# Masked products, longer paces, and low parts of weights made by adding DMAs in a decoder trunk's first phase

## The chip, the cores and the metric

The kernel runs on one core of a Trainium2 chip. The metric is the device time of one execution in microseconds (us); less is better. TensorE (PE) multiplies matrices, VectorE (DVE), ScalarE (ACT) and GpSimd (POOL) work element by element, and SyncE (SP) issues most DMAs. Each engine runs its own queue in order and waits on semaphores of the others.

## The reference

One layer of a decoder on 512 tokens with 2048 features, all in float32:

```
u = rmsnorm(h, ln_mix);  z = u @ w_in
out_a = RG-LRU of z[:, :2048]          # 8 tiles of 128 channels: conv, two gates, a scan, norm
out_b = RWKV-7 of z[:, 2048:]          # 16 heads of 64, a recurrence over the tokens
h = h + concat(out_a, out_b) @ w_o
h = h + (gelu(conv(u @ w_gate)) * (u @ w_up)) @ w_down
h = h + rmsnorm(sigmoid(u @ w_ple_gate) * (p @ w_ple_proj));  result = rmsnorm(h)
```

The RWKV recurrence is done here in chunks of 64 tokens. In a chunk, the dependence of a token on the earlier ones is a triangular system, so each chunk of each head needs the inverse of a unit triangular 64x64 matrix.

## The kernel before

**Dense products.** Each float32 operand is split into a high part, rounded to the format that TensorE takes at full rate (float32r), and a low part, the rest. A product takes three matmuls: high by high, high by low, low by high (L151, L153, L155 in `dense`). Weights come in units, mostly 128x8x128: `wfill_` has SP load a unit to `wraw` (two buffers), ACT make the high part `whi` (L121) and DVE the low part `wlo` = raw - high (L122). There are three buffers for the pair, and units are prepared two ahead of their use. A unit of eight blocks feeds 24 matmuls of 512 columns.

**Phases.** Phase 1 does w_in, the LRU, the RWKV heads and most of w_o; phase 2 the rest of w_o, the feed-forward block and the embedding gate. The `NB` first output blocks of w_o take the first half of the RWKV rows already in phase 1 ("wob", after the point "out6", where head pair 6 must be done) and the second half in phase 2.

**Order on TensorE in phase 1.** It is written out by `merge`, which interleaves a stream of dense matmuls with generators for the eight head pairs: `prep` (decays, keys, in six steps), `batch` (scores and inverses), `chain` (the recurrence over eight chunks) and `norm`. `merge` keeps a clock t of its own. A dense matmul adds 216, and a step of a generator adds the `pe` that it yields; its next step is due when t has passed the `lat` that it yields. These come from the table `W`: `t0` after the start of the inverses, `tg` and `tt` between their levels, `lu` and `ls` in the chain, `dpace` and `pace` as the least distance of the steps of a duo (chain of pair j-1 beside batch of pair j; `dpace` for pairs 1 to 7), `g2` and `g3` for the norm, `late` and `ready` for the start of a duo, `dec` and `rsk` in prep. Since the order is fixed, TensorE waits where an operand is late, also if other matmuls could run.

**Order on the other engines.** A scheduler orders them by priority; `high_priority(offset=...)` moves a block ahead. `offw` is for the weights' conversions, `offs` for the heads' core, `offd` for what follows a dense product, `offl` for the LRU, `offt` for transposes by DVE within the core, `offp` for the steps of prep.

**Start of the inverses** (in `batch`, L755 to L762): from the scores MQ, four products (one for each group of 32 partitions) with the mask `lev1`, an add of the identity and a 32x32 transpose give Tt and Tm for the first level. The next step of TensorE on them is L768.

**Prep's second step** (L624 to L636): ACT squares k (L624), TensorE makes two small products, ACT takes tanh; `head_ss` (L905) then sums the squares on TensorE. `norm` has the same L905, GpSimd's power (L915), a copy on DVE (L917) and transposes on TensorE (L924).

Of the kernel before, what the change touches and what calls it, by code (L numbers as in the profile page):

```python
# [4 lines left out]
F32 = mybir.dt.float32  # L5
F32R = mybir.dt.float32r
AF = mybir.ActivationFunctionType
ALU = mybir.AluOpType
# [3 lines left out]
D = 2048  # L12
S = 512
KT = D // 128
NB = 6

W = dict(offw=10000, offp=[0, 5000, 1000, 2000, 5000, 5000, 1000], offl=10000, offt=100, pace=155, dpace=2794, late=4073, offs=17427, offd=2000, start=2297, lora=2383, dec=0, rsk=12597, ready=23343, bonus=39298, t0=4838, tg=1911, tt=1448, lx=14094, lu=1308, ls=1058, g1=8521, g2=4936, g3=6474, per=[2, 3, 2, 2, 2, 2, 3, 0])
DL = 1024
NP = 8
FF = 6144  # L20
# [16 lines left out]
for _n, _c in PCOLS:  # L37
# [2 lines left out]
PW = _o  # L40

CCOLS = [("ident", 128), ("ones1", 1), ("mask", 128)] + [("lev1", 32)] + [("lev%d" % b, 16) for b in (2, 4, 8, 16)] + \
        [("bdm", 128), ("bd2", 2), ("id32", 32)]
CKEEP = 129
COFF = {}
_o = 0
# [6 lines left out]
def shape_constants():  # L53
    c = np.zeros((128, CW), np.float32)
    p = np.arange(128)
    s = p % 64
    t = np.arange(64)
    c[:, COFF["ident"]:COFF["ident"] + 128] = np.eye(128)
    o = COFF["mask"]
    c[:, o:o + 64] = s[:, None] < t[None, :]  # L60
    c[:, o + 64:o + 128] = s[:, None] <= t[None, :]

    r = (p % 32)[:, None]
    t = np.arange(32)[None, :]
    c[:, COFF["lev1"]:COFF["lev1"] + 32] = (t // 2 == r // 2) & (t % 2 == 1) & (r % 2 == 0)

    for b in (2, 4, 8, 16):
        o = COFF["lev%d" % b]
        c[:, o:o + 16] = ((r // b) % 2 == 1) & (r // (2 * b) == t[:, :16] // b)
    o = COFF["id32"]  # L70
    c[:, o:o + 32] = r == t
    o = COFF["bdm"]
    c[:, o:o + 128] = (p[:, None] // 64 == p[None, :] // 64) / 64.0
    o = COFF["bd2"]
    c[:, o:o + 2] = p[:, None] // 64 == np.arange(2)[None, :]
    c[:, COFF["ones1"]] = 1.0
    return c


class Builder:  # L80
# [22 lines left out]
    def wfill_(self):  # L103
        nc = self.nc
        while self.wn < len(self.wq) and len(self.wt) < self.LOOK:
            src, shape, *own = self.wq[self.wn]
            self.wn += 1
            if callable(src):
                raw = src()
            elif self.wraw:  # L110
                raw = self.wraw.pop(0)
            else:
                raw = self.t(self.cp, "wraw", shape, bufs=self.RAW)
                nc.sync.dma_start(raw, src)
            if own:
                w = self.t(self.k2, own[0], (128, 2) + shape[1:], F32R, bufs=1)
                hi, lo = w[:, 0], w[:, 1]
            else:
                hi = self.t(self.wp, "whi", shape, F32R, bufs=self.HL)
                lo = self.t(self.wp, "wlo", shape, F32R, bufs=self.HL)  # L120
            nc.scalar.activation(hi, raw, AF.Copy)  # L121
            nc.vector.tensor_tensor(lo, raw, hi.bitcast(F32), ALU.subtract)  # L122
            self.wt.append((hi, lo))

    def wnext(self):
# [75 lines left out]
    def build(self):  # L201
        nc, tc, A = self.nc, self.tc, self.A
        self.RAW, self.HL, self.LOOK = 2, 3, 2
        self.PACE, self.OFFS, self.OFFD = W["pace"], W["offs"], W["offd"]
        from contextlib import ExitStack
        with ExitStack() as top:

            cp = top.enter_context(tc.tile_pool(name="cp", bufs=1, side="right"))
            self.cp = cp
            self.par = cp.tile([128, PW], F32, name="par")  # L210
            self.con = cp.tile([128, CKEEP], F32, name="con")
            self.mug1 = cp.tile([32, 1], F32, name="mug1")
            self.mhalf = cp.tile([128, 8], F32, name="mhalf")
            nc.gpsimd.memset(self.mhalf, -0.5)
            self.wp = top.enter_context(tc.tile_pool(name="wp", bufs=1))
            self.dp = top.enter_context(tc.tile_pool(name="dp", bufs=1, space=DRAM))
            self.bp = top.enter_context(tc.tile_pool(name="bp", bufs=1))
            self.oa = [self.dp.tile([128, S], F32, name="oa%d" % i) for i in range(8)]
            self.ob = [self.dp.tile([128, S], F32, name="ob%d" % i) for i in range(8)]
            self.rsa = cp.tile([128, S], F32, name="rsa")  # L220
            with ExitStack() as ph:
                self.pm = ph.enter_context(tc.tile_pool(name="pm1", bufs=1, space=PSUM))
                self.k1 = ph.enter_context(tc.tile_pool(name="k1", bufs=1))
                self.phase1()
            with ExitStack() as ph:
                self.pm = ph.enter_context(tc.tile_pool(name="pm2", bufs=1, space=PSUM))
                self.k2 = ph.enter_context(tc.tile_pool(name="k2", bufs=1))
                self.phase2()
# [372 lines left out]
    def prep(self, j):  # L601
        nc, A, k1 = self.nc, self.A, self.k1
        V, SC, G, TE = nc.vector, nc.scalar, nc.gpsimd, nc.tensor
# [7 lines left out]
        raw = T("lraw", 1, (128, 4, 128))  # L611
# [21 lines left out]
        SC.activation(th, th, AF.Tanh, scale=-E05 / 4, bias=self.cq[:, 0:1])  # L633
        ta = T("ta")
        SC.activation(ta, psa, AF.Tanh, scale=0.5, bias=self.dv("a0h", j))
        yield 860, W['dec']  # L636

        ss = self.head_ss(sq)
        V.tensor_scalar(th, th, -1.0, 1.0, ALU.mult, ALU.add)
# [12 lines left out]
        rsk = self.head_bc(mb)  # L652
# [10 lines left out]
        ready = self.now + W['ready']  # L663
# [10 lines left out]

        G.tensor_tensor(rt, rt, kt, ALU.mult)
        bdr = T("bdr", 1, (128, 128))
        V.tensor_scalar(bdr, self.K("bdm"), self.P("rk", j), 64.0, ALU.mult, ALU.mult)
        bv = T("bv", 2)
        self.prepped[j] = (AR, bt, ktl, vt, pc, bv, gt)
        self.ptime = max(ready, self.now + W['late'])  # L680
# [26 lines left out]
    def batch(self, j, q):  # L707
        nc, A, k1 = self.nc, self.A, self.k1
        V, SC, G, TE = nc.vector, nc.scalar, nc.gpsimd, nc.tensor
# [8 lines left out]
        MQ, NQ = T("MQ", 2, (128, NC, 128)), T("NQ", 2, (128, NC, 128))  # L718
# [36 lines left out]
        Q4 = [(slice(32 * g, 32 * g + 32), slice(32 * (g % 2), 32 * (g % 2) + 32)) for g in range(4)]  # L755
        Tm, Tt = T("Tm", 1, (128, 8, 32)), T("Tt", 1, (128, 8, 32))
        bc = lambda n, w: self.K(n).unsqueeze(1).broadcast_to([128, 8, w])
        for r_, c_ in Q4:
            V.tensor_tensor(Tt[r_], MQ[r_, :, c_], bc("lev1", 32)[r_], ALU.mult)
        V.tensor_tensor(Tt, Tt, bc("id32", 32), ALU.add)  # L760
        V.transpose(fl(Tm), fl(Tt))
        yield 2160, W['t0']  # L762

# [365 lines left out]
    def phase2(self):  # L1129
        nc, A, k2 = self.nc, self.A, self.k2  # L1130
        V, SC, G, TE = nc.vector, nc.scalar, nc.gpsimd, nc.tensor
        self.MM = 6
        self.auxtag = ("wk", 2)
        T = lambda tag, bufs=1, shape=(128, S), dt=F32: self.t(k2, tag, shape, dt, bufs)
        self.obs.append(self.last)
# [3 lines left out]
        for m in range(KT):  # L1139
# [3 lines left out]
            hi, lo = T("uh%d" % m, dt=F32R), T("ul%d" % m, dt=F32R)  # L1143
# [30 lines left out]
        raw = [None, None]  # L1174
# [145 lines left out]
        for k in range(2):  # L1320
            r = T("ld")
            nc.sync.dma_start(r, A["pT"][k])
            t_ = T("hw%d" % (4 + k), 1, (128, 2, 512), F32R)
# [178 lines left out]
```

## Time and profile before

| | us |
|---|---|
| median of 3 runs (lowest to highest) | 2706.22 (2706.09 to 2706.65) |
| profiled execution | 2707.82 |
| its span, first to last instruction | 2706.0 |
| TensorE busy | 2646.9 |
| VectorE busy | 1735.8 |
| ScalarE busy | 1051.0 |
| GpSimd busy | 291.1 |

The profile's mean granted TensorE clock is 0.99 of 2.4 GHz. A busy TensorE counts from an instruction's start to its modelled end, and consecutive matmuls overlap: a matmul of 512 columns is listed at some 390 to 400 ns. The idle time before an instruction is put down to the semaphore that ended it last ("<- engine, tile, line").

### The profile page before, as it was taken

The numbers are of one execution on the slowest core, as the hardware profiler recorded it, in microseconds if no ns is written. First come the engines' busy times: TensorE is split into PE (matmuls) and PEld (weight loads), VectorE is DVE, ScalarE is ACT, GpSimd is POOL, SyncE is SP. The second block draws the span as 40 slices with busy tenths as digits, with TensorE's granted clock in tenths as the row PEclk, the third lists the DMA queues.
The fourth block names the chain that finished last, engine by engine and source line by source line (L and its number), as shares of the span: only waits on it lengthen the run. The fifth ranks groups of instructions, "written<-read, shape, count | busy, mean of one in ns | idle before, by whom it ended". The sixth has DMA issues, their size and how long they took to land.

```text
span 2706.0 us, 43401 instructions
## 1 busy us (share of the span) xinstructions
PE 2646.9 (98%) x18440; PEld 2175.3 (80%) x18440; DVE 1735.8 (64%) x2321; ACT 1051.0 (39%) x1483; POOL 291.1 (11%) x217
## 2 busy tenths in 40 slices
PE   8999999999999999999999999999999999999996
PEld 7877777787787788888888888888888888888886
DVE  7774866677574634666666667667666667775235
ACT  6453454446432433333333333333333333335244
POOL 4010110101121310000000000000000000000013
PEclk9999999999999999999999999999999999999998
DMA  5221221222242422323323323232233323332322
GB/s 174 90 75 57 83 75 52 80 83 68 91 141 75 133 93 86 102 99 107 100 101 109 102 94 107 93 104 95 100 109 101 109 94 101 101 107 85 101 86 102
DMA packets 81890, 261.35 MB, mean 97 GB/s; under 512 B 9504, under 2 KB 12192, under 8 KB 81696
## 3 DMA queue, kind: packets, MB, share of 16 engines
q1 hardware_dynamic: 81696, 258.58, 28.9%
q8 instruction: 144, 2.36, 0.4%
q14 instruction: 50, 0.41, 0.0%
HBM read 250.42 MB, written 8.13 MB: 96 GB/s over the span
## 4 chain that ended last, share of the span: by engine, by line
PE 90%; DVE 5%; ACT 2%; POOL 1%; issue 1%; DMA 1%; SPq 0%; DVEq 0%; POOLq 0%
PE wk L1171 12%; PE wk L1170 12%; PE wk L1172 12%; PE mm L155 7%; PE mm L153 7%; PE mm L151 7%; PE mm L1253 6%; PE mm L1252 6%; PE mm L1254 6%; PE mm L1341 2%; PE mm L1339 2%; PE mm L1340 2%; PE wk L768 2%; PE mm L1170 1%; PE mm L1172 1%; PE mm L1171 1%
## 5 line engine op out<-in xcount | busy, mean ns | idle before, releaser
L121 ACT ACTIVATE whi<-wraw 128x1024 fp32r<-128x1024 f32 (+2 forms) x361 | 375.2, 1039 | 744.6 <-PE mm L153 195.7
L122 DVE TENSOR_TENSOR wlo<-wraw,whi 128x1024 fp32r<-128x1024 f32 (+2 forms) x361 | 444.7, 1232 | 225.9 <-ACT whi L121 220.2
L1170 PE MATMUL wk<-uh,whi 128*128 128x512 f32 x1408 | 547.8, 389 | 0.0
L1171 PE MATMUL wk<-ul,whi 128*128 128x512 f32 x1408 | 547.7, 389 | 0.0
L1172 PE MATMUL wk<-uh,wlo 128*128 128x512 f32 x1408 | 547.7, 389 | 0.0
L121 ACT ACTIVATE whi<-hw 128x1024 fp32r<-128x1024 f32 x154 | 163.3, 1061 | 464.5 <-PE wk L1171 418.5
L151 PE MATMUL mm<-xh,whi 128*128 128x512 f32 x832 | 333.7, 401 | 1.5 <-DVE y L888 0.9
L155 PE MATMUL mm<-xh,wlo 128*128 128x512 f32 x832 | 333.6, 401 | 1.5 <-DVE wlo L122 1.5
L153 PE MATMUL mm<-xl,whi 128*128 128x512 f32 x832 | 333.2, 401 | 0.0
L1172 PEld LDWEIGHTS wk<-uh,wlo 128*128 128x128 f32 x1408 | 264.3, 188 | 54.9
L1170 PEld LDWEIGHTS wk<-uh,whi 128*128 128x128 f32 x1408 | 264.3, 188 | 54.9
L1171 PEld LDWEIGHTS wk<-ul,whi 128*128 128x128 f32 x1408 | 264.3, 188 | 54.8
L122 DVE TENSOR_TENSOR wlo<-hw,whi 128x1024 fp32r<-128x1024 f32 x154 | 188.7, 1225 | 181.0 <-ACT whi L121 178.5
L1253 PE MATMUL mm<-wlo,hid 128*128 128x512 f32 x680 | 265.1, 390 | 0.0
L1254 PE MATMUL mm<-whi,hid 128*128 128x512 f32 x680 | 264.8, 389 | 0.0
L1252 PE MATMUL mm<-whi,hid 128*128 128x512 f32 x680 | 264.8, 389 | 0.0
L1198 POOL TENSOR_TENSOR tmp<-tmp,rsa 128x512 f32<-128x512 f32 x48 | 87.4, 1821 | 1361.0 <-ACT tmp L1197 1361.0
L151 PEld LDWEIGHTS mm<-xh,whi 128*128 128x128 f32 x832 | 158.5, 190 | 37.4 <-issue 3.7
L155 PEld LDWEIGHTS mm<-xh,wlo 128*128 128x128 f32 x832 | 158.0, 190 | 37.3 <-issue 2.8
L153 PEld LDWEIGHTS mm<-xl,whi 128*128 128x128 f32 x832 | 158.4, 190 | 34.2 <-issue 1.3
L1267 DVE TENSOR_TENSOR h<-h,mm 128x512 f32<-128x512 f32 x264 | 175.2, 682 | 0.6
L1252 PEld LDWEIGHTS mm<-whi,hid 128*128 128x128 f32 x680 | 127.6, 188 | 26.4
(468 smaller groups left out, 3648.3 us busy)
## 6 DMA issues: line engine op xcount, KB each, us to landing
wraw<-wgu SPq DMA_DIRECT2D x192, 512.0 KB, 3.2
hw<-wd SPq DMA_DIRECT2D x88, 512.0 KB, 3.2
wraw<-wz SPq DMA_DIRECT2D x80, 512.0 KB, 3.5
wraw<-wpg SPq DMA_DIRECT2D x31, 512.0 KB, 3.2
wraw<-wo SPq DMA_DIRECT2D x24, 512.0 KB, 3.4
wraw<-wo SPq DMA_DIRECT2D x16, 256.0 KB, 2.8
tmp<-xT SPq DMA_DIRECT2D x16, 256.0 KB, 2.8
wraw<-wd SPq DMA_DIRECT2D x8, 512.0 KB, 3.2
```

What stands on the lines that cost most here:

```text
L121: nc.scalar.activation(hi, raw, AF.Copy)
L122: nc.vector.tensor_tensor(lo, raw, hi.bitcast(F32), ALU.subtract)
L151: nc.tensor.matmul(ps, hi[:, k, :], xh, start=first and i == 0, stop=False)
L153: nc.tensor.matmul(ps, hi[:, k, :], xl, start=False, stop=False)
L155: nc.tensor.matmul(ps, lo[:, k, :], xh, start=False, stop=last and i == n - 1)
L1170: TE.matmul(ps, wh[:, k, :], xh, start=h + k == 0, stop=False)
L1171: TE.matmul(ps, wh[:, k, :], xl, start=False, stop=False)
L1172: TE.matmul(ps, wl[:, k, :], xh, start=False, stop=h == 1 and k == 7)
L1252: TE.matmul(ps, x[0][:, k, ts_], w[0][:, k, :], start=first and k == 0, stop=False)
L1253: TE.matmul(ps, x[0][:, k, ts_], w[1][:, k, :], start=False, stop=False)
L1254: TE.matmul(ps, x[1][:, k, ts_], w[0][:, k, :], start=False, stop=last and k == 1)
L1267: V.tensor_tensor(o, o, ps[tt], op)
```

## The change

Five things change.

1. The start of the inverses takes two products on all 128 partitions instead of four on 32. Each has a mask by partition (`odd`, a new constant of two columns) beside `lev1`; an add of the identity and an add of the two results follow. Also, `bdr` is made from `bd2`, and the constant `bdm` is dropped.
2. `NB` goes from 6 to 8, so two more half blocks of w_o are done in phase 1.
3. The table `W` has new values: longer `t0`, `dpace`, `ls`, `late`, `lora`, `g3`, `pace`, shorter `tg` and `start`, and other offsets for the priorities.
4. A new `dec7` is the distance between prep's second and third step for the last head pair, where `dec` is 0 for all others.
5. In phase 1 (`acc_lo`), every other unit of shape 128x8x128 gets its low part in another way: ACT writes the negated high part to `wlo`, and a DMA issued by GpSimd adds the weights from DRAM to it. DVE has no part in it. Space for GpSimd's DMA descriptors is doubled.

```
-NB = 6
-W = dict(offw=10000, offp=[0, 5000, 1000, 2000, 5000, 5000, 1000], offl=10000, offt=100, pace=155, dpace=2794, late=4073, offs=17427, offd=2000, start=2297, lora=2383, dec=0, rsk=12597, ready=23343, bonus=39298, t0=4838, tg=1911, tt=1448, lx=14094, lu=1308, ls=1058, g1=8521, g2=4936, g3=6474, per=[2, 3, 2, 2, 2, 2, 3, 0])
+NB = 8
+W = dict(offw=3000, offp=[0, 300, 0, 1000, 5000, -100, 466], offl=0, offt=0, pace=1007, dpace=3159, late=8560, offs=10000, offd=3000, start=1554, lora=5885, dec=0, rsk=12832, ready=23343, bonus=39298, t0=5900, tg=1601, tt=1464, lx=4233, lu=1319, ls=1435, g1=97321, g2=4936, g3=7972, per=[2, 3, 2, 2, 2, 2, 3, 0], dec7=6140)
...
+    c[:, COFF["odd"]:COFF["odd"] + 2] = p[:, None] // 32 % 2 == np.arange(2)[None, :]
...
             nc.scalar.activation(hi, raw, AF.Copy)
-            nc.vector.tensor_tensor(lo, raw, hi.bitcast(F32), ALU.subtract)
+            if self.acc_lo and not callable(src) and shape == (128, 8, 128) and self.wn % 2:
+                nc.scalar.activation(lo, hi.bitcast(F32), AF.Copy, scale=-1.0)
+                nc.gpsimd.dma_start(lo, src, accum_op=ALU.add)
+            else:
+                nc.vector.tensor_tensor(lo, raw, hi.bitcast(F32), ALU.subtract)
...
-        yield 860, W['dec']
+        yield 860, W['dec'] if j < NP - 1 else W['dec7']
...
-        V.tensor_scalar(bdr, self.K("bdm"), self.P("rk", j), 64.0, ALU.mult, ALU.mult)
+        V.tensor_scalar(bdr.rearrange("p (h f) -> p h f", h=2), self.K("bd2").unsqueeze(2).broadcast_to([128, 2, 64]), self.P("rk", j), None, ALU.mult)
...
-        for r_, c_ in Q4:
-            V.tensor_tensor(Tt[r_], MQ[r_, :, c_], bc("lev1", 32)[r_], ALU.mult)
-        V.tensor_tensor(Tt, Tt, bc("id32", 32), ALU.add)
+        for i, t_ in enumerate((Tm, Tt)):
+            V.scalar_tensor_tensor(t_, MQ[:, :, 32 * i:32 * i + 32], self.K("odd")[:, i:i + 1], bc("lev1", 32), ALU.mult, ALU.mult)
+        V.tensor_tensor(Tm, Tm, bc("id32", 32), ALU.add)
+        V.tensor_tensor(Tt, Tt, Tm, ALU.add)
         V.transpose(fl(Tm), fl(Tt))
...
-    nc = _bacc.Bacc("TRN2", target_bir_lowering=False, num_devices=1, dynamic_dma_scratch_size=512)
+    nc = _bacc.Bacc("TRN2", target_bir_lowering=False, num_devices=1, dynamic_dma_scratch_size=1024)
```

## Rows read from the trace of the kernel before

**Rows 1.** Stretches: start:end, length, busy of PE PEld DVE ACT POOL; clock, DMA.
```profile
36.00:890.00 854.00, 823.53 (x10094) 656.23 (x10094) 562.08 (x944) 388.84 (x639) 112.17 (x87) 0.98 0.26 81
890.00:2686.00 1796.00, 1791.83 (x8153) 1491.60 (x8151) 1131.78 (x1331) 629.88 (x783) 149.88 (x93) 1.00 0.30 101
```

**Rows 2.** Waits of PE, 44 to 890 us: total us, times, longest us.
```profile
PE wk L768 <- DVE Tm L761: 6.8, 2, 5.1
PE wk L768 <- DVE us L849: 3.3, 2, 2.1
PE wk L905 <- ACT tmp L624: 3.0, 1, 3.0
PE wk L924 <- DVE Sq L917: 2.9, 1, 2.9
PE wk L924 <- DVE MQ L728: 1.8, 2, 1.1
...
PE mm L155 <- DVE wlo L122: 1.5, 1, 1.5
...
PE wk L726 <- DVE bt L657: 0.9, 1, 0.9
```

**Rows 3.** Stretches around three of the six places of low clock.
```profile
317.00:321.50 4.50, 4.50 (x86) 3.78 (x87) 3.98 (x7) 0.09 (x1) 3.43 (x3) 0.62 0.27 81
...
733.50:741.50 8.00, 7.57 (x23) 6.37 (x24) 6.35 (x10) 1.43 (x2) 1.64 (x1) 0.57 0.20 45
...
884.00:891.00 7.00, 5.57 (x15) 4.24 (x16) 3.19 (x5) 1.44 (x2) 0.04 (x1) 0.51 0.04 16
```

**Rows 4.** PE in order of time (start us, us): dense matmuls three apart.
```profile
879.78 0.39 PE L155 MATMUL mm<-xh,wlo 128*128 128x512 f32 x1
...
880.46 0.40 PE L155 MATMUL mm<-xh,wlo 128*128 128x512 f32 x1
```

**Rows 5.** Groups of DVE by line, 36 to 890 us: count, busy us, mean ns.
```profile
L759 DVE TENSOR_TENSOR Tt<-MQ,con 32x256 f32<-32x256 f32 x32 | 13.8, 430 | 0.5
...
L760 DVE TENSOR_TENSOR Tt<-Tt,con 128x256 f32<-128x256 f32 x8 | 3.2, 406 | 0.1
```

**Rows 6.** DVE in order of time: one scalar_tensor_tensor.
```profile
494.29 0.74 DVE L442 SCALAR_TENSOR_TENSOR kt<-zs,par,tmp 128x512 f32<-128x512 f32 x1
```

**Rows 7.** PE in order of time, chunks of the last chain ahead of "out6".
```profile
853.31 0.33 PE L847 MATMUL ch<-st,MQ 64*64 64x64 f32 x4 [0.21 <-DVE st L870]
853.47 0.28 PE L853 MATMUL ch<-vk,kk 64*64 64x64 f32 x4
...
855.30 0.33 PE L847 MATMUL ch<-st,MQ 64*64 64x64 f32 x4 [0.88 <-DVE st L870]
```

**Rows 8.** Groups by line, 36 to 860 us: the conversions of weights.
```profile
L121 ACT ACTIVATE whi<-wraw 128x1024 fp32r<-128x1024 f32 x97 | 102.6, 1058 | 151.1 <-PE mm L153 143.9 <-issue 5.3 <-PE ch L862 0.8
...
L122 DVE TENSOR_TENSOR wlo<-wraw,whi 128x1024 fp32r<-128x1024 f32 x97 | 129.0, 1330 | 32.5 <-ACT whi L121 31.5 <-PE wk L193 0.5 <-PE mm L155 0.2
```

**Rows 9.** DMA issues, 50 to 860 us: count, KB each, median us to landing.
```profile
wraw<-wz SPq DMA_DIRECT2D x75, 512.0 KB, 3.5
```

**Rows 10.** Groups of POOL by line, 36 to 860 us: its longest op.
```profile
L983 POOL TENSOR_TENSOR lxl<-lxl,lrc 128x512 f32<-128x512 f32 x4 | 8.4, 2106 | 27.2 <-DVE us L849 9.2 <-ACT bk L746 6.9 <-DVE lrc L598 6.4
```

**Rows 11.** ACT and PE in order of time: two units, high part and low part's use.
```profile
30.80 1.06 ACT L121 ACTIVATE whi<-wraw 128x1024 fp32r<-128x1024 f32 x1 [1.20 <-DMA wraw<-wz]
...
36.55 0.40 PE L155 MATMUL mm<-xh,wlo 128*128 128x512 f32 x1
...
473.30 1.07 ACT L121 ACTIVATE whi<-wraw 128x1024 fp32r<-128x1024 f32 x1
...
481.72 0.39 PE L155 MATMUL mm<-xh,wlo 128*128 128x512 f32 x1
```

**Rows 12.** DVE and POOL in order of time, 481 to 484 us.
```profile
481.60 2.04 DVE L122 TENSOR_TENSOR wlo<-wraw,whi 128x1024 fp32r<-128x1024 f32 x1
...
481.27 1.29 POOL L983 TENSOR_TENSOR lt<-lt,lrc 128x512 f32<-128x512 f32 x1 [7.21 <-ACT lxl L977]
```

More of the change, by code (lines that the diff above doesn't have):

```diff
@@ L42 @@
 CCOLS = [("ident", 128), ("ones1", 1), ("mask", 128)] + [("lev1", 32)] + [("lev%d" % b, 16) for b in (2, 4, 8, 16)] + \
-        [("bdm", 128), ("bd2", 2), ("id32", 32)]
+        [("bd2", 2), ("id32", 32), ("odd", 2)]
 CKEEP = 129
@@ L71, in shape_constants @@
     c[:, o:o + 32] = r == t
-    o = COFF["bdm"]
-    c[:, o:o + 128] = (p[:, None] // 64 == p[None, :] // 64) / 64.0
     o = COFF["bd2"]
@@ L203, in build @@
         self.RAW, self.HL, self.LOOK = 2, 3, 2
+        self.acc_lo = True
         self.PACE, self.OFFS, self.OFFD = W["pace"], W["offs"], W["offd"]
@@ L1132, in phase2 @@
         self.MM = 6
+        self.acc_lo = False
         self.auxtag = ("wk", 2)
```

## The prediction

> **What bounds the kernel now.** I began with the four long stretches of the span. After 890 us TensorE is busy for 1791.8 of 1796.0 us, so nothing the change touches can be won there; from 36 to 890 us (all of phase 1 behind its start) it is idle for 854.0 - 823.5 = 30.5 us, with VectorE busy for 562 us and ScalarE for 389 us of the 854 [rows 1]. Phase 1's TensorE order is fixed in the program, so each such idle time is an operand that came late. Next I read who ended TensorE's waits there: most were ended by VectorE, few are longer than 1 us, and the largest are at the start of the triangular inverses (L768: 6.8 us in two waits, 3.3 us in two more), in prep 7 (L905, 3.0 us, ended by ScalarE) and in the last head's norm (L924, 2.9 us) [rows 2]. Behind a wait there is a second price: the granted clock of the stretches around the waits at 317, 734 and 884 us is 0.62, 0.57 and 0.51, a mix of the levels 2.4 and 1.2 GHz after TensorE had been idle [rows 3] (the wait at 493 us has the same 0.62 behind it; of such stretches there are six in phase 1). A share c over w us means 2(1-c)w us at 1.2 GHz: 3.4, 6.9 and 6.9 us, where each busy us does half its work. So the prize in phase 1 is some 30 us of waits and some 10 us of clock; all else is matmuls that stay.
>
> **How positions in the order follow.** merge() adds 216 per dense matmul and the (pe, lat) of each yield to a clock t, and the next step comes when t has passed lat. So a constant is a number of matmuls between two steps: t0=4838 is 4838/216, 23 matmuls, t0=5900 is 28. In the trace three dense matmuls take 0.68 us (879.78 to 880.46), 0.227 us each [rows 4]. Stepping t through with either set of constants gives all the counts below.
>
> **Edit 1, masked products and t0.** Before, VectorE does four products on 32 partitions (0.43 us each) and an add (0.41): 4 x 0.43 + 0.41 = 2.13 us [rows 5], then a transpose. After, two products on all partitions, two adds, and the same transpose. That product (scalar_tensor_tensor, 256 columns) isn't in the trace: it lies between 0.43 us (256 columns, two inputs) and 0.74 us (the same instruction at 512 columns) [rows 5, 6], so the four are 1.7 to 2.3 us; I take 0.43, as the add on 128 partitions costs no more than the product on 32. Saved: 0.45 us, or lost: 0.2 us. Between the scores and L768 there are now 28 matmuls for 23 (25 for 20 in some heads): 5 x 0.227 = 1.13 us. Each of the four waits shrinks by 1.58 us: 5.1 to 3.5, 1.7 to 0.1, 2.1 to 0.5, 1.2 to 0 [rows 2]: 6.0 us gained. The low clock behind the second and third goes too: 2 x 3.4/2 = 3.4 us [rows 3]. Together **-9.4 us** (0 to -13).
>
> **Edit 2, dec7.** In prep 7, L905 follows the tanh step with no matmul between, and waits 3.0 us for ScalarE's L624 [rows 2]. With 6140 there are 17 matmuls between, 3.9 us: the wait goes, and its low clock with it, 6.9/2 = 3.4 us [rows 3]. **-6.4 us** (-3 to -6.4).
>
> **Edit 3, g3 and NB=8.** Before, no matmul is left between L905 and L924 of the last norm, which waits 2.9 us; now 24 matmuls (two w_o units) move ahead of phase 2, 17 of them between the two: 3.9 us of cover. The 24 are the same work either way. With the wait goes the low clock: TensorE is busy for 5.6 us of that stretch, at half rate, 2.8 us at most, of which I take 2.1 us, since its start is the small transposes of L924 [rows 3]. The 0.9 us for y L888 stays. **-5.0 us** (-2 to -5).
>
> **Edit 4, dpace, ls, late and the other paces.** Steps of heads 1 to 7 now stand 15 matmuls apart, not 13; prep's first step gets 16 to 19 (not 12), norms 25 to 37 (not 21 to 30). pace 155 to 1007 does nothing worth naming: the waits of its duos are longer anyhow. That covers the waits for bt at L726 and MQ at L924 (0.9 and 1.8 us) [rows 2]: **-2.7 us** (0 to -4, with two more for Sq and Tm, under 1 us each). But the heads' work ends later against the dense work. The dense stream stops at "out6" after 2473 matmuls in both; before, five core steps follow without a matmul between them, now nine (two of duo 7, seven of duo 8). Two such steps take 855.30 - 853.31 = 2.0 us there [rows 7]; 1.0 us of it is TensorE's own work, there anyhow: six groups of four small matmuls, 0.16 us from one to the next [rows 7]. Four more steps cost 2 x 1.0 = 2.0 us, and about as much low clock again as behind a 3 us wait rather than a 2 us one: (6.9 - 3.4)/2 = 1.7 us [rows 3]. **+3.7 us** (+2 to +8).
>
> **Edit 5, low parts by DMA.** It concerns 49 units (every other one of 84 w_in and gate units, and of 14 w_o units). Each takes a subtraction of 1.33 us off VectorE (65 us in all) and puts a second ScalarE pass of 1.06 us in (52 us; ScalarE goes from 389 to 441 of 854 us) [rows 1, 8], a DMA issue on GpSimd, and 512 KB more. GpSimd's queue is in order: pow for the norms and the LRU's products queue behind an issue that waits for ScalarE's pass; the norms now have at least 25 matmuls (5.7 us) for that. The low part is now ready at: high part's end + 1.06 + issue + landing. Landing isn't in the trace: not under the plain 512 KB load, 3.5 us; since an add reads both operands and writes, I bound it by two such passes, 7.0 us [rows 9]. The issue costs GpSimd between nothing and its longest two-input op (2.1 us), and can stand behind one such op [rows 10]. So 4.6 to 12.3 us; I take 1.06 + 1.0 + 5.0 = 7.1. Against this stands the time from a high part's end to the first matmul on its low part. It is shortest for the first unit, 31.86 to 36.55 = 4.7 us, then 474.37 to 481.72 = 7.4 us [rows 11]; worked out so for all 49, the next are 8.3, 8.9 and 9.1, the median is 15.3. At 7.1 one unit is late: **+2.4 us**. At 12.3, thirteen are, by 40 us. ScalarE's bursts already made a high part late once (L155 on wlo, 1.5 us [rows 2]); one more of these: **+1.5 us**.
>
> The plain load's 3.5 us says what one pass costs, not two [rows 9]. The Trainium skill (Collectives: The Full Stack, "The bandwidth ceiling") says that a DMA's add costs not its arithmetic but a second read; with the fit of its page DMA: Bandwidth & Descriptors ("Anatomy of one DMA", 2.0 us + bytes/436e3) an estimate is 2.0 + 2 x 1.2 = 4.4 us for landing, and by that the first unit would be late by 1.8 us. No run so far shows an adding DMA.
>
> GpSimd and VectorE hinder each other here: a wlo that began at 481.60 us beside GpSimd's L983 took 2.04 us [rows 12], 0.7 us over the mean of 1.33 [rows 8]. If each issue did so, 49 x 0.7 = 34 of the 65 us off VectorE would be given back. The Trainium skill (SBUF — State Buffer, "SBUF: two separate sides") has a rule for it, that whichever of the two starts first holds the shared port pair for its whole instruction; the trace agrees. No row shows whether an issue does this.
>
> **The sum.** -9.4 - 6.4 - 5.0 - 2.7 + 3.7 + 2.4 + 1.5 = -15.9 us. Against the profiled execution's 2707.82 us (span 2706.0 and 1.8 around it) that is 2691.9; the median of the runs, 2706.22, is 1.6 lower: **2690 us**, for itself 2679 to 2702 (terms at their ends, not all at once).
>
> **Rivals.**
> First, late low parts (slower). Place: L155 at the start of a DMA-fed unit. For it: three passes in a row over queues that were short of time once already, and ScalarE and GpSimd at the front of them. Against it: the median of 15.3 us. At 12.3 us: 40 us late instead of 2.4, and eleven of the waits over 1.5 us, each with 1.7 us of clock, 19: 2690 - 2 + 40 + 19 = 2747 us. It decides from about 10 us, where eight units are late by 13.5 us and the clock takes 5.
> Second, the waits move. Each engine's queue is ordered anew by the offsets (weights 3000, conversions of dense results 3000, LRU 0), and a wait such as that for Tm hangs on what VectorE's queue puts between its five steps. Then edits 1 and 4 give nothing and the rest -6.4 - 5.0 + 3.7 + 2.4 + 1.5 = -3.8: 2702 us.
> Third, VectorE with 65 us less to do lets the remaining waits go as well: the 3.5 us left of the first wait at L768 and the 1.5 us for wlo [rows 2], the 1.5 us allowed for ScalarE, and a low clock of the 6.9 us kind behind the first of these, 3.4 us: 9.9 us more, 2680 us. It asks for all of VectorE's relief and no new wait on ScalarE.
>
> **How the numbers follow.** Forecast 0.53, late low parts 0.17, moved waits 0.15, more gone 0.15. Range 2674 to 2716: it leaves out most of the first rival (0.13) and a tail below (0.05). A measurement of this kernel tells about 0.2% (5.4 us) from no change. Faster by more: forecast and third rival, and a part of the second, 0.68; within: 0.14; slower: 0.18.
>
> **What would show it.** Right: no wait at L905 for L624 or at L924 of the last norm; clock 1.0 at the places of 317, 493, 734 and 886 us; waits at L768 under 4 us in sum; idle of 36 to 890 us near 17 us; a longer bare stretch before "out6". Wrong: waits at L151 or L155 ended by a DMA into wlo, landing above 8 us, GpSimd's pow late, or a VectorE that is no less busy.

## The result, and the profile after

The changed kernel takes **2688.32 us** (median; 2686.98 to 2690.18) against 2706.15 us before on the same chip: ratio 0.9935, 95% interval 0.9917 to 0.9952. Its profiled execution has a span of 2686.2 us, 19.8 less than before's. One execution below (of the kernel with the paces and offsets alone) took 4177.74 us at a mean clock of 0.58 and is left out; all others are of the fast state.

Lines of after stand a little lower in the code: L122 is now L127 (L124 is ScalarE's negated copy, L125 the adding DMA), L151/L153/L155 are L156/L158/L160, L624 is L630, L657 is L663, L728 is L734, L759 to L761 are L765 to L768, L768 is L775, L905 is L912, L917 is L924, L924 is L931.

First the stretches of after, with the columns of [rows 1] (busy of PE, PEld, DVE, ACT, POOL; granted clock, share of the DMA engines, GB/s); the second ends where phase 2's first matmul starts.

```profile
36.00:890.00 854.00, 833.83 (x10182) 668.12 (x10181) 522.44 (x907) 439.93 (x698) 155.47 (x138) 0.99 0.45 115
...
36.00:873.70 837.70, 817.55 (x10110) 654.72 (x10109) 508.59 (x890) 430.88 (x684) 151.46 (x135) 0.99 0.44 113
```

TensorE idles 20.2 us in 36 to 890 us, where it idled 30.5 [rows 1]. Phase 2's first matmul starts at 873.73 us, before at 886.55, and by then 24 more matmuls are done (24 x 0.227 = 5.4 us, [rows 4]). So phase 1 gives 12.8 + 5.4 = 18.2 us, and what follows 1.6 us. Of the 18.2, the idle time up to that point is 10.2 (before, 36 to 886.5 us: 850.5 - 820.1 = 30.4 us; after: 837.7 - 817.6 = 20.2 us). The other 8 are busy time: 2.5 us less of it, with 5.4 us more work in it. Part of those 8 is the clock: from 36 us to phase 2 it is recorded at 0.5 for 29.6 us before and 20.5 us after, and half of the difference is 4.6 us. The other 3.4 us weren't traced further.

Places of low clock, after. The first three and the fifth are those of the prediction (317, 493, 734 and 884 us before [rows 3], the last now 866 to 880 us); the fourth and the sixth are two of the three where it is low now.

```profile
317.00:321.50 4.50, 4.50 (x72) 3.77 (x61) 3.75 (x6) 0.00 (x0) 0.00 (x0) 1.00 0.32 103
494.50:499.00 4.50, 4.50 (x100) 3.54 (x99) 4.08 (x7) 2.22 (x4) 0.81 (x1) 1.00 0.52 158
733.50:741.50 8.00, 8.00 (x41) 6.58 (x39) 7.62 (x11) 2.55 (x5) 1.29 (x1) 1.00 0.41 135
835.00:846.00 11.00, 9.55 (x121) 7.91 (x117) 4.51 (x13) 2.21 (x5) 1.66 (x1) 0.69 0.01 2
866.00:880.00 14.00, 12.36 (x61) 10.09 (x60) 8.17 (x15) 4.42 (x7) 1.64 (x1) 1.00 0.27 95
38.00:46.00 8.00, 5.57 (x21) 4.54 (x21) 3.48 (x11) 4.93 (x11) 5.25 (x5) 0.57 0.74 185
```

The prediction's four are at full clock. Left are the stretches behind the waits at 40 and 207 us (the latter's clock is 0.74 over 201 to 214 us) and the bare steps before "out6" (835 to 846 us). The waits of TensorE, 36 to 890 us (total us, times, longest):

```profile
PE mm L160 <- DMA wlo<-wz: 7.1, 2, 3.8
PE wk L775 <- DVE Tm L768: 4.9, 2, 4.2
PE mm L156 <- DVE y L895: 1.6, 1, 1.6
...
PE mm L160 <- DMA wlo<-wo: 0.7, 1, 0.7
```

Against [rows 2]: the waits for ScalarE's squares (3.0 us), for Sq in the last norm (2.9), for us at the inverses (3.3) and for bt (0.9) are gone, and of those for MQ (1.8) 0.2 is left; of the inverses' waits 4.9 us is left, nearly all at one place (207.55 us, 4.17 us). New are low parts that come late by DMA, 7.8 us in three.

Groups of DVE, ACT and POOL by line, 36 to 890 us (count, busy us, mean ns; then the idle time ahead):

```profile
L127 DVE TENSOR_TENSOR wlo<-wraw,whi 128x1024 fp32r<-128x1024 f32 x49 | 65.0, 1326 | 18.8 <-ACT whi L121 18.4 <-PE mm L160 0.3
...
L765 DVE SCALAR_TENSOR_TENSOR Tm<-MQ,con 128x256 f32<-128x256 f32 x8 | 3.8, 471 | 0.2
...
L124 ACT ACTIVATE wlo<-whi 128x1024 fp32r<-128x1024 f32 x48 | 50.6, 1054 | 2.0 <-issue 1.2
L125 POOL DMA_DIRECT2D wlo<-wz x39 | 34.8, 891 | 328.2 <-ACT wlo L124 254.5 <-DVE us L856 19.7 <-DVE Gm L785 15.3
```

DMA issues (KB each, median us to landing) and queues (packets, MB, share of 16 engines), 30 to 860 us:

```profile
q1 hardware_dynamic: 25120, 68.46, 25.9%
q0 software_dynamic: 7056, 25.69, 18.3%
...
wraw<-wz SPq DMA_DIRECT2D x78, 512.0 KB, 3.6
wlo<-wz POOLq DMA_DIRECT2D x40, 512.0 KB, 5.6
```

So the parts of edit 5 cost about what was taken: ScalarE's pass 1.05 us, and 5.6 us (5.0 to 8.1) to landing. The time to landing counts from the start of the issue, so the issue's 0.89 us of GpSimd are part of it: the first issue starts at 33.80 us, lands 6.6 us later, and TensorE goes on at 40.43 us. Chain: 1.05 + 5.6 = 6.7 us where 7.1 was taken.

### The profile page after: what moved, and what is told of

It reads as the page before. It is cut to its first block, busy times and chain, and to the rows that moved or that the text cites. A ratio compares the mean times of both kernels' runs of the same rounds, so it can differ in the third digit from the quotient of the medians.

```text
span 2686.2 us, 43499 instructions
## 1 busy us (share of the span) xinstructions
PE 2636.5 (98%) x18440; PEld 2170.1 (81%) x18440; DVE 1684.7 (63%) x2268; ACT 1096.7 (41%) x1532; POOL 328.5 (12%) x266
## 3 DMA queue, kind: packets, MB, share of 16 engines
q0 software_dynamic: 7056, 25.69, 5.7%
## 4 chain that ended last, share of the span: by engine, by line
PE 91%; DVE 4%; DMA 2%; ACT 1%; POOL 1%; issue 1%; SPq 0%; DVEq 0%; POOLq 0%; ACTq 0%
PE wk L1178 12%; PE wk L1180 12%; PE wk L1179 12%; PE mm L160 7%; PE mm L158 7%; PE mm L156 7%; PE mm L1262 6%; PE mm L1260 6%; PE mm L1261 6%; PE mm L1348 2%; PE mm L1349 2%; PE mm L1347 2%; PE wk L775 2%; PE mm L1178 1%; PE mm L1180 1%; PE mm L1179 1%
## 5 line engine op out<-in xcount | busy, mean ns | idle before, releaser
L127 DVE TENSOR_TENSOR wlo<-wraw,whi 128x1024 fp32r<-128x1024 f32 (+2 forms) x314 | 380.6, 1212 | 213.4 <-ACT whi L121 208.5
L160 PE MATMUL mm<-xh,wlo 128*128 128x512 f32 x832 | 333.5, 401 | 7.1 <-DMA wlo<-wz 7.1
L156 PE MATMUL mm<-xh,whi 128*128 128x512 f32 x832 | 331.2, 398 | 1.6 <-DVE y L895 1.6
L158 PE MATMUL mm<-xl,whi 128*128 128x512 f32 x832 | 330.5, 397 | 0.0
L127 DVE TENSOR_TENSOR wlo<-hw,whi 128x1024 fp32r<-128x1024 f32 x154 | 188.6, 1225 | 181.2 <-ACT whi L121 178.8
L160 PEld LDWEIGHTS mm<-xh,wlo 128*128 128x128 f32 x832 | 156.9, 189 | 42.2 <-DMA wlo<-wz 8.0
L156 PEld LDWEIGHTS mm<-xh,whi 128*128 128x128 f32 x832 | 157.1, 189 | 35.8 <-issue 4.5
L158 PEld LDWEIGHTS mm<-xl,whi 128*128 128x128 f32 x832 | 157.0, 189 | 34.1 <-issue 2.0
L1261 PEld LDWEIGHTS mm<-wlo,hid 128*128 128x128 f32 x680 | 127.6, 188 | 26.4
```

Of the source, the lines that this page charges most:

```text
L156: nc.tensor.matmul(ps, hi[:, k, :], xh, start=first and i == 0, stop=False)
L158: nc.tensor.matmul(ps, hi[:, k, :], xl, start=False, stop=False)
L160: nc.tensor.matmul(ps, lo[:, k, :], xh, start=False, stop=last and i == n - 1)
L1261: TE.matmul(ps, x[0][:, k, ts_], w[1][:, k, :], start=False, stop=False)
```

## The experiments

Twelve kernels, each timed beside the kernel before on the same chip, whose median there was 2706.5 to 2706.8 us. "After" stands for the changed kernel. Kernels that go back to the table of before keep the new `bdr`, the constants and the descriptor space of after.

### The paces and offsets alone

After with DMA low parts off (`acc_lo`) and the four old products at the start of the inverses.

```
-        self.acc_lo = True
+        self.acc_lo = False
...
+        for r_, c_ in Q4:
+            V.tensor_tensor(Tt[r_], MQ[r_, :, c_], bc("lev1", 32)[r_], ALU.mult)
+        V.tensor_tensor(Tt, Tt, bc("id32", 32), ALU.add)
```

> The changed kernel with the old inverses (four products on 32 partitions) and all low parts by VectorE: the new table, dec7 and NB=8 alone. Theory 'cover' (the gain is the matmuls put between steps): edits 2, 3 and 4 and the 1.13 us of t0 in edit 1 stay, the 2.4 + 1.5 us of late low parts go, so 2688 to 2696 us, with no wait at L905 for ScalarE's squares and none at the last L924. Theory 'relief' (the gain is VectorE's 65 us less of low parts): most waits stay or move, 2699 to 2708 us.

Measured 2686.00 us (median of five executions), 0.9930 (0.9916 to 0.9943), 2 us under the low end of theory 'cover'. The new table (with `dec7`) and `NB` alone give the whole gain; neither the masked products nor the DMAs are needed for it. Its waits are other ones, though, of about the same sum (TensorE idles 18.1 us in 36 to 890 us, in after 20.2):

```profile
PE wk L930 <- DVE MQ L734: 3.4, 2, 2.6
PE wk L774 <- DVE Tm L767: 3.2, 2, 2.0
PE wk L732 <- DVE bt L663: 2.5, 1, 2.5
PE wk L198 <- POOL rsr L189: 2.1, 1, 2.1
```

### The DMA low parts alone

The kernel before (its table, `NB`, products) with edit 5.

```
+        self.acc_lo = True
...
+            if self.acc_lo and not callable(src) and shape == (128, 8, 128) and self.wn % 2:
+                nc.scalar.activation(lo, hi.bitcast(F32), AF.Copy, scale=-1.0)
+                nc.gpsimd.dma_start(lo, src, accum_op=ALU.add)
```

> The kernel before, with every other 128x8x128 unit's low part made by an adding DMA; table, NB and inverses as before. Theory 'cover': the waits of before stay but for the part that VectorE's shorter queue takes off, and the first unit's late low part comes on top, so 2702 to 2712 us. Theory 'relief': VectorE gives back the waits that it ended (some 20 us less 4 to 8 us of late low parts), 2688 to 2698 us. Landing near 5.6 us as in the changed kernel in both.

Measured 2731.40 us, 1.0093 (1.0080 to 1.0106): 25 us slower, outside both expectations. VectorE does have less to do (507 us busy of 854, before 562 [rows 1]). But the waits at the start of the inverses grow from 10.1 us before (the two L768 lines of [rows 2]) to 25 (24.8, and 0.4 for us):

```profile
PE wk L774 <- DVE Tm L767: 24.8, 4, 8.4
PE mm L160 <- DMA wlo<-wz: 10.5, 3, 4.9
```

VectorE's queue at the longest of them, in order of time (start us, us):

```profile
676.55 1.28 DVE L734 TENSOR_TENSOR MQ<-wk,con 128x512 f32<-128x512 f32 x2
...
679.05 1.86 DVE L765 TENSOR_TENSOR Tt<-MQ,con 32x256 f32<-32x256 f32 x2
...
681.88 2.57 DVE L604 RECIPROCAL lrc<-lrc 128x128 f32<-128x128 f32 x3
...
684.45 0.94 DVE L604 RECIPROCAL lrc<-lrc 128x128 f32<-128x128 f32 x1
...
685.96 1.36 DVE L765 TENSOR_TENSOR Tt<-MQ,con 32x256 f32<-32x256 f32 x1
...
688.86 0.42 DVE L765 TENSOR_TENSOR Tt<-MQ,con 32x256 f32<-32x256 f32 x1
689.32 1.22 DVE L994 TENSOR_TENSOR_SCAN lxl<-lrc,lxl 128x512 f32<-128x512 f32 x1
690.46 0.40 DVE L766 TENSOR_TENSOR Tt<-Tt,con 128x256 f32<-128x256 f32 x1
690.89 0.45 DVE L767 STREAM_TRANSPOSE Tm<-Tt 128x256 f32<-128x256 f32 x1
```

The operand takes 13.5 us from the scores' end on VectorE (677.8) to Tm (691.3), because an LRU tile's four reciprocals, a scan and the norm's products stand between its own six operations. This is what the next runs look into.

### The masked products alone

The kernel before with edit 1's products (`t0` as before).

```
-        for r_, c_ in Q4:
-            V.tensor_tensor(Tt[r_], MQ[r_, :, c_], bc("lev1", 32)[r_], ALU.mult)
-        V.tensor_tensor(Tt, Tt, bc("id32", 32), ALU.add)
+        for i, t_ in enumerate((Tm, Tt)):
+            V.scalar_tensor_tensor(t_, MQ[:, :, 32 * i:32 * i + 32], self.K("odd")[:, i:i + 1], bc("lev1", 32), ALU.mult, ALU.mult)
+        V.tensor_tensor(Tm, Tm, bc("id32", 32), ALU.add)
+        V.tensor_tensor(Tt, Tt, Tm, ALU.add)
```

> The kernel before with the masked products alone. The four instructions took 0.47 + 0.74 + 0.42 + 0.52 us = 2.1 us in the changed kernel, as long as the five before (2.13 us), so the two waits of 5.1 and 1.7 us at L768 should stay within 0.5 us: 2703 to 2708 us by both theories; below 2700 would mean that the number of instructions in VectorE's queue matters more than their time.

Measured 2702.93 us, 0.9985 (0.9977 to 0.9994): 3.9 us under before (2706.82), just past the low end of what was expected. The four waits at L775 are 4.47, 1.05, 1.39 and 0 us, where before had 5.11, 1.71, 2.05 and 1.26: 0.65 us less for the first three (up to 0.5 was expected), and the fourth gone. The low clock behind the second and third is gone as well, but two others come, at 350 and 470 us.

### All but the DMA low parts

```
-        self.acc_lo = True
+        self.acc_lo = False
```

> The changed kernel with all low parts by VectorE, all else kept. Theory 'cover': the DMA edit cost 7.8 us of late low parts on TensorE (3.8, 3.3, 0.7), so without it 2680 to 2688 us, less what VectorE's 65 us bring back as waits. Theory 'relief': VectorE is short again, 2694 to 2704 us, with more waits ended by VectorE than in the changed kernel.

Measured 2687.26 us, 0.9929 (0.9918 to 0.9941), which is after's own time within the intervals: in the new table edit 5 is worth nothing that shows. VectorE is busy for 575.0 us of 36 to 890 (after 522.4), ScalarE for 394.6 (439.9). Where after waits for DMA low parts, this kernel waits for other things:

```profile
PE wk L931 <- DVE MQ L734: 3.4, 2, 2.6
PE wk L732 <- DVE bt L663: 2.5, 1, 2.5
PE mm L555 <- ACT vk L541: 2.5, 2, 1.8
PE wk L198 <- POOL rsr L189: 2.2, 1, 2.2
PE wk L775 <- DVE Tm L768: 1.9, 2, 1.4
```

The 2.5 us for vk are at 40 to 42 us, just where after waits 3.8 us for its first DMA low part.

### Undoing dec7

```
-dec7=6140
+dec7=0
```

> The changed kernel with dec7=0, so that L905's sums (now L912) of the last pair follow the tanh step at once. Theory 'each wait has its cover' (a constant pays where a wait of before stood): the 3.0 us wait for ScalarE's squares and its low clock come back, +6.4 us, 2693 to 2696 us. Rival 'the table as a whole' (offsets and order decide, single constants are interchangeable): within 3 us of the changed kernel, 2686 to 2691 us. Something is given back too: prep 7 and so duo 7 come 17 matmuls earlier, and the bare steps ahead of out6 get fewer, -2 us.

Measured 2690.83 us, 0.9940 (0.9928 to 0.9953): 2.5 us over after, not 6.4 (and the two intervals overlap), as the rival expected. There is no matmul between the tanh step and L912 again, and still no wait for the squares: in the new order ScalarE has them done earlier.

### Undoing the end

`NB` and `g3` as before.

```
-NB = 8
+NB = 6
...
-g3=7972
+g3=6474
```

> The changed kernel with NB=6 and g3=6474: two w_o half blocks fewer after out6 and none between the last norm's two steps. Theory 'each wait has its cover': the wait of 2.9 us at L924 (now L931) and its low clock of 2.1 us come back, 2692 to 2695 us. Rival: 2686 to 2691 us.

Measured 2689.95 us, 0.9942 (0.9930 to 0.9955): 1.6 us over after, within the intervals and the rival's range, 2 us short of the theory's. And yet the wait comes back, to the hundredth before's 2.91 us, with low clock behind it:

```profile
867.56 1.11 PE L931 MATMUL wk<-con,Sq 128*128 128x128 f32 x4 [2.91 <-DVE Sq L924]
869.54 0.76 PE L156 MATMUL mm<-xh,whi 128*128 128x512 f32 x1 [0.87 <-DVE y L895]
```

But its longest other waits are new as well: after's low part that is 3.3 us late at 306 us isn't late here, while 1.7 and 1.8 us waits stand elsewhere (at L775 and L931).

### Undoing t0

```
-t0=5900
+t0=4838
```

> The changed kernel with t0=4838: 23 matmuls, not 28, between the scores and the first step of the inverses. Theory 'each wait has its cover': waits at L768 (now L775) grow by 1.1 us each, from 4.2 + 0.7 us in two to some 9 us in four or more, and two or three of them bring low clock (1.7 to 3.4 us each), 2695 to 2702 us. Rival: 2686 to 2692 us.

Measured 2726.93 us, 1.0075 (1.0062 to 1.0088): **38.6 us** over after and slower than before, where 7 to 14 us were expected.

```profile
PE wk L775 <- DVE Tm L768: 23.7, 6, 9.7
...
PE mm L156 <- ACT lt L979: 4.0, 1, 4.0
```

In the longest of these waits (9.7 us, head 4) four reciprocals of an LRU tile stand on VectorE in the middle of the operand's own steps, from 494.5 to 499.1 us.

### Undoing dpace and ls

```
-dpace=3159 ... ls=1435
+dpace=2794 ... ls=1058
```

> The changed kernel with dpace=2794 and ls=1058: steps of heads 1 to 7 13 matmuls apart, not 15. Theory 'each wait has its cover': some small waits of the norms and preps come back (2.7 us) but the bare steps ahead of out6 go from nine back to five or fewer (-3.7 us), so about even, 2685 to 2691 us. Rival (a longer pace is what takes the waits off everywhere): 2694 to 2704 us.

Measured 2721.54 us, 1.0056 (1.0043 to 1.0070): **33 us** over after; both expectations missed. The number of matmuls between the scores and L775 is after's (44 or 45 TensorE operations in heads 1 to 6), and yet:

```profile
PE wk L775 <- DVE Tm L768: 21.3, 4, 7.6
```

VectorE's queue at the longest of them, from the scores' last product to Tm, holds an LRU tile's four reciprocals and its scan ahead of the operand's own steps:

```profile
487.83 0.69 DVE L734 TENSOR_TENSOR MQ<-wk,con 128x512 f32<-128x512 f32 x1 [1.01 <-PE wk L732]
...
489.37 3.38 DVE L604 RECIPROCAL lrc<-lrc 128x128 f32<-128x128 f32 x4
...
496.76 1.21 DVE L995 TENSOR_TENSOR_SCAN lxl<-lrc,lxl 128x512 f32<-128x512 f32 x1
...
501.44 0.45 DVE L768 STREAM_TRANSPOSE Tm<-Tt 128x256 f32<-128x256 f32 x1
```

Nor do the bare steps ahead of "out6" get fewer, as was expected: TensorE has no dense matmul for 14.4 us there (861.2 to 875.6), in after for 12.6, in before for 6.2.

### The old offsets

```
-offw=3000, offp=[0, 300, 0, 1000, 5000, -100, 466], offl=0, offt=0
+offw=10000, offp=[0, 5000, 1000, 2000, 5000, 5000, 1000], offl=10000, offt=100
...
-offs=10000, offd=3000
+offs=17427, offd=2000
```

> The changed kernel with the priority offsets of before (offw, offl, offt, offs, offd and offp), paces, DMA lows and masked products kept: the same order on TensorE, another on the other engines. Theory 'offsets' (LRU at 0 keeps its operations out of the inverses' first steps, and prep's squares early): more than 3 us of VectorE's other work comes between the scores and Tm in heads 3, 5 and 7 and the 3.0 us wait for ScalarE's squares may return, 2700 to 2725 us. Theory 'paces' (the TensorE order alone): 2686 to 2694 us.

Measured 2706.24 us, 1.0002 (0.9992 to 1.0011). Without the new offsets nothing of the gain is left. The time is as expected, the way isn't: the inverses wait at one place only, and there is no wait for the squares (`dec7` covers them). What came instead is a dense matmul that waits 9.2 us, at 478 us, for a tanh of the LRU's gate on ScalarE, and three late low parts.

```profile
PE mm L160 <- DMA wlo<-wz: 9.5, 3, 3.5
PE mm L156 <- ACT lt L979: 9.2, 1, 9.2
PE wk L775 <- DVE Tm L768: 4.3, 1, 4.3
```

### Old dpace without the LRU's reciprocals

The kernel of "Undoing dpace and ls", and the LRU's four reciprocals per tile left out, with another scaling in their place (so out_a is not the reference's).

```
-            V.tensor_scalar(rc, t1, -1.0, 1.0, ALU.mult, ALU.add)
+            V.tensor_scalar(rc, t1, 0.25, 0.75, ALU.mult, ALU.add)
...
-            self.recip(r3, r3)
```

> The kernel with dpace=2794 and ls=1058 (2721.5 us), with the LRU's four reciprocals per tile left out (a scaling stands in their place, so the LRU's decays and the output are not the reference's). There, VectorE's other work between the scores and Tm was 11.5 us in the head at 488 us and 7.5 us in that at 676 us, 3.6 and 3.7 us of each the LRU's reciprocals, and TensorE waited 7.6 and 5.7 us. Theory 'collision' (the pace only decides whether the LRU's tile stands in VectorE's queue when an inverse starts): those two waits fall below 3 us each and the time to 2698 to 2710 us. Theory 'pace' (longer steps cover waits everywhere): only VectorE's share falls, the waits stay within 2 us, 2714 to 2721 us.

Measured 2702.95 us, 0.9990 (0.9981 to 0.9999): 18.6 us less than with them. Of the four waits at L775 (3.89, 4.08, 7.58, 5.71 us) 0, 1.01, 0 and 0.61 are left. That VectorE has less to do as such doesn't explain it: with 52 us less (after against "All but the DMA low parts") the time stays. Of the 33 us that the old `dpace` and `ls` cost, 14.6 remain here. Its longest waits:

```profile
PE mm L160 <- DMA wlo<-wz: 8.4, 3, 3.1
...
PE wk L775 <- DVE us L856: 1.0, 1, 1.0
```

### Old t0 without the DMA low parts

```
-t0=5900
+t0=4838
...
-        self.acc_lo = True
+        self.acc_lo = False
```

> The changed kernel with t0=4838 and all low parts by VectorE. With DMA lows t0=4838 cost 38.6 us. Theory 'the adding DMAs set off the collisions' (with them the order on VectorE puts the LRU and the norm ahead of the inverse's steps; without them not): waits at the inverses' start as in the kernel before less 0.4 us, 2690 to 2700 us. Theory 't0 alone': as with DMA, 2715 to 2730 us.

Measured 2718.69 us, 1.0058 (1.0043 to 1.0072): 31.4 us over the same kernel with the new `t0` (2687.26). So it isn't the DMAs that make `t0` matter so much; that theory falls.

```profile
PE wk L775 <- DVE Tm L768: 12.6, 5, 6.1
...
PE wk L775 <- DVE us L856: 4.5, 1, 4.5
```

### A shorter least distance in the last duo

```
-                    cr = t + max(lat, W['dpace'] if 0 < cj < NP else self.PACE)
+                    cr = t + max(lat, (W['dpace'] if cj < NP - 1 else 2000) if 0 < cj < NP else self.PACE)
```

> The changed kernel with a least distance of 2000 instead of 3159 in duo 7 alone, where the LRU is done: its chain ends 32 matmuls earlier, and ahead of out6 four or five steps stand without a matmul, not nine. Theory 'bare steps' (edit 4's price, about 1 us for two steps and the low clock of 6.8 us that follows): 2683 to 2686 us, with the stretch from the last dense matmul to the first behind out6 shorter by some 4 us. Rival (duo 7's own steps wait instead, as steps nine matmuls apart leave ScalarE and VectorE too little): 2688 to 2694 us.

Measured 2687.36 us, 0.9932 (0.9919 to 0.9945), 1.0 us under after, within its interval, and between the two ranges expected. Two stretches of it, and the second in after:

```profile
829.00:846.00 17.00, 16.09 (x149) 11.77 (x149) 8.22 (x19) 4.73 (x9) 5.11 (x3) 1.00 0.22 70
305.00:312.00 7.00, 5.48 (x51) 4.65 (x51) 4.02 (x7) 6.82 (x11) 2.14 (x2) 0.52 0.84 238
```

```profile
305.00:312.00 7.00, 5.58 (x61) 4.62 (x62) 5.59 (x11) 6.90 (x11) 2.15 (x2) 1.00 0.83 236
```

The place before "out6" did what it should: no low clock there (after 0.69), one wait of 0.9 us, and phase 2's first matmul comes 104.5 us after head 7's scores are on VectorE, where after has 107.8. But behind the late low part at 306 us (3.54 us here, 3.31 in after) the clock is 0.52 in this execution, where it is 1.00 in after, although TensorE's order up to there is the same in both. With 5.5 us of work in that stretch, half of it undone by that clock, this takes some 2.7 us of the gain back.

## Why the prediction was right in sum and wrong in its terms

The time came out 1.7 us from the forecast, and the account of what was bounded holds: the gain lies in phase 1 (18.2 of 19.8 us), 14.8 us of it in waits and low clock, and the two waits singled out at L905 and L924 went together with their clock. The prices of the single edits don't hold, so that their sum came out as near as this is luck. One count was short: the prediction names six places of low clock and sets some 10 us for them, but from 36 us to phase 2 the trace of before has seven (the first at 41 us), and half of their 29.6 us is 15.

**Edit 1 and the step that failed.** For one wait at the start of the inverses, three times can be read from the trace: from the end of the scores on TensorE to MQ, from MQ to Tm on VectorE, and the cover, that is when TensorE got through the matmuls between. The operand's time is the sum of the first two; what it exceeds the cover by is the wait. Operand time in us, with the cover in brackets:

| | head 1 | head 2 | head 4 | head 6 |
|---|---|---|---|---|
| before | 11.15 (6.1) | 7.71 (6.1) | 7.77 (5.9) | 7.63 (6.5) |
| after | 11.34 (7.2) | 6.40 (7.1) | 6.92 (7.0) | 7.98 (7.4) |
| old `t0` | 8.89 (6.1) | 11.00 (6.2) | 15.24 (5.7) | 8.84 (5.9) |
| old `t0`, no DMA | 8.56 (6.6) | 10.21 (5.9) | 13.27 (7.3) | 7.40 (5.9) |
| old `dpace` | 11.05 (7.2) | 11.25 (7.2) | 14.10 (6.7) | 12.57 (7.0) |
| old `dpace`, no reciprocals | 6.50 (7.2) | 8.09 (7.2) | 6.05 (6.6) | 7.93 (7.5) |

Both sizes that were worked out are there. The cover grew by 1.1 us in heads 1 and 2, as stepped through. Where VectorE does nothing else in between, MQ to Tm takes 2.19 us, before 2.68: 0.49 us less, for 0.45 forecast. And head 1's wait, 4.2 us, is near the 3.5 forecast. The products alone, in the order of before, also do what was worked out: 0.65 us off each wait. What failed is the sentence "Each of the four waits shrinks by 1.58 us": the four shrink by 0.9, 1.7, 2.0 and 0.6 us, in sum by 5.2 for 6.0, but that is how this set of constants falls out. The sentence keeps the operand time fixed while the order changes. Between 6 and 15 us that time is set by what stands ahead on VectorE, and that changes with every constant that moves the heads against the dense matmuls and the LRU tiles. With the old `dpace` the cover is after's, and the operand times of heads 2, 4 and 6 are 4.6 to 7.2 us longer: the waits at L775 are 21.3 us in sum for 4.9, and that comes from the operand times alone. That it is the queue is shown by the run without reciprocals, 18.6 us faster, with the same order on TensorE and the operand times of heads 4 and 6 back at 6.05 and 7.93 us. (In heads 1 and 2 no reciprocal stood between MQ and Tm; the shortening there is before MQ, and the run doesn't separate what of it comes from the shorter queue and what from the heads standing elsewhere again. In head 2 the four reciprocals stood just ahead of MQ, 307.8 to 311.4 us.) Head 1's wait, the one that is left in after, is of another kind: VectorE isn't busy ahead of MQ but idle, as its queue stands at a transpose that waits for ScalarE's copies:

```profile
200.56 0.71 DVE L753 STREAM_TRANSPOSE kk<-kk 128x512 f32<-128x512 f32 x1 [5.35 <-ACT kk L752]
```

**The moved waits, with the opposite sign.** The second rival said that a wait for Tm hangs on VectorE's queue between its steps. That mechanism is the one that decides here; the rival took it to cost some 12 us of the gain, in fact the new constants as a set avoid collisions (an operand's steps behind an LRU tile's on VectorE) which undoing `t0` or `dpace` alone brings back. One at a time, undoing costs 38.6 (`t0`), 33 (`dpace`, `ls`), 17.9 (offsets), 2.5 (`dec7`) and 1.6 us (end), 94 us together of a change that is worth 17.8 in all. So terms of such a table don't add up, and a sum of them that comes out right, as here, says little about each. The low clock is a third to a half of each large one. From 36 us to phase 2 TensorE idles 43.5 us with the old `t0`, 41.8 with the old `dpace` and 29.7 with the old offsets (after: 20.2), and the clock is at 0.5 for 44.4, 47.8 and 41.0 us (after: 20.5). The added idle time and half of the added low clock make 35, 35 and 20 us, where the profiled executions are longer by 34, 32 and 18.

**Edit 2.** The wait went, and its low clock with it (clock 1.00 in 733.5 to 741.5 us). It was laid to `dec7` for 6.4 us; undoing `dec7` costs 2.5, not clear of the noise, with no squares waited for when it is undone, and none either with the old offsets and `dec7` kept. So `dec7` suffices, and so does the rest of the new table without it; the prediction saw only the first.

**Edit 3.** The mechanism is the best seen of all: undone, the same 2.91 us wait returns with its low clock. Only 1.6 us of the 5.0 show in the time (bounds 2 to 5). Of the rest, 0.8 us is the wait for y behind it (0.87 before, 1.64 after: with Sq earlier, y is next, which the prediction left at 0.9); the others go into what undoing the end changes elsewhere (the late low part of 3.3 us that goes, the two waits of 1.7 and 1.8 us that come), and that wasn't taken apart.

**Edit 4.** The bare stretch before "out6" was forecast at +3.7 us; taking it away gave 3.4 us between head 7's scores and phase 2. That price was about right, but not its cause: with `dpace` and `ls` undone the stretch is no shorter (14.4 us for 12.6), and which of the other constants made it stays open. The waits it was to cover (bt, MQ) are gone in after, but for 0.2 us, and not without the DMAs: 2.5 and 3.4 us. So the longer distance alone doesn't cover them: with it and the same order on TensorE they come to 5.9 us where VectorE makes all low parts.

**Edit 5.** Forecast +3.9 us, in the table of after nothing: after less "all but DMA" is +1.1 us, within the intervals. Three low parts are late by 7.8 us in sum, not one by 2.4. The first: seven small operations of GpSimd stand ahead of the issue (32.0 to 33.8 us, where ScalarE's pass ends at 33.1), and this landing took 6.6 us. The second stands at 306 us, where the new order lets ScalarE's high part end at 298.6 us, 4.5 us ahead of its use; in the order of before no unit but the first had under 7.4 us [rows 11], so the list of 49 was worked out for an order that was gone. They show nothing in the time because other waits go in exchange: the first stands in place of the waits for vk (2.5 us) and rsr (2.2 us) of the kernel without DMAs, and that kernel's 2.5 and 3.4 us for bt and MQ are but 0.2 us in after. In the table of before the same edit costs 25 us (the run with DMAs alone). That is far more than the late low parts (10.5 us), the first rival's mechanism; of the waits that come, the larger part (15 us) is at the inverses.

The adding DMA takes 18.3% / 25.69 MB = 0.71% of the DMA engines per MB against 25.9% / 68.46 = 0.38%, 1.9 times as much. The Trainium skill (Collectives: The Full Stack, "The bandwidth ceiling") puts the cost of a DMA's add in its second read; the trace agrees with a factor near two, though the two kinds also go through different queues (q0 software, q1 hardware), and no run separates the add from that. The estimate of landing that the prediction made from the fit of the Trainium skill (DMA: Bandwidth & Descriptors, "Anatomy of one DMA"), 4.4 us, is 1.2 us short of the measured 5.6; from the end of the issue the measured time is 4.7.

**GpSimd's issues and VectorE.** If each of 49 issues had held VectorE for 0.7 us, 34 of the 65 us would have come back. VectorE is busy 575.0 - 522.4 = 52.5 us less than in the same kernel with subtractions, whose 97 take 127.5 us where after's 49 take 65.0, 62.5 less: 10 us came back, 0.21 per issue. How much of it is the issues and how much the other order isn't separated. (In [rows 12] the two engines' instructions overlap by 0.96 us, and VectorE's took 0.7 longer than its mean: the trace agrees only roughly with the rule that the prediction cites from the Trainium skill, SBUF — State Buffer, "SBUF: two separate sides".)

**The signs.** Right: no wait for the squares or for the last Sq, clock 1.00 at the four places, the longer bare stretch. Short: idle 20.2 us for 17, and 4.9 us of waits at L775 for under 4. Of the signs of wrong, waits for DMA into wlo came (7.8 us), and one landing in the run's list reached 8.1 us, the median staying at 5.6.

**What stays open.** The values of `late`, `lora`, `ls`, `lu`, `tg` and the single offsets weren't separated. Nor is it known why VectorE's scheduler puts the LRU ahead of the inverses in one order and behind in the other; only where it does is shown. And no run is clearly under after: 2686.00 (paces alone), 2687.26 (all but DMAs) and 2687.36 us (short last duo) have intervals that overlap its own.

## What to carry to other kernels

Where TensorE's order is written out and the other engines' queues are ordered by a scheduler, a constant isn't worth its matmuls of cover: read the operand's own time from the trace (last producer to ready) with everything that stands between on the producing engine, and ask what a shift puts there. Test such a table by undoing one constant at a time; where the parts sum to several times the whole, the table works as an alignment and not as a list of savings, and an edit that is harmless in one table (here the DMAs) may cost 25 us in another. Taking work off an engine that isn't the bound gave nothing here in itself: 52 us less of VectorE moved the time by nothing measurable (2688.32 against 2687.26 us).

## What the runs showed of the hardware

An adding DMA from HBM into SBUF of 512 KB lands 5.6 us after the start of its issue (5.0 to 8.1), a plain load of the same size in 3.6 us, and its issue takes 0.86 to 1.03 us of GpSimd. After a TensorE wait at 306 us, the same place in the same order, the clock over 305 to 312 us was 1.00 in one execution (after, 3.31 us of wait) and 0.52 in another (short last duo, 3.54 us); the wait of 2.91 us at the end of before has 0.51 behind it [rows 3]. So the length of the idle time alone doesn't tell its price. The masked product (scalar_tensor_tensor, 128x256) takes 0.47 us where nothing disturbs it, near the lower of its bounds of 0.43 and 0.74.
